# Gated linear attention with decays as per-token factors, grown block by block, two chunks per step

## The chip, the cores and the metric

The kernel runs on one core of a Trainium2 chip. The metric is the device time of one execution in microseconds (us), taken as the median of several timed runs. The core's engines are TensorE (PE in the rows; PEld is its loading of weights), VectorE (DVE), ScalarE (ACT), Pool (POOL) and SyncE (SP), which here only issues transfers. Each engine works through its own queue in order.

## The reference

One layer over 256 context tokens and 1024 latent tokens, width 1024. After a modulated norm one projection of 3616 columns feeds two groups of four heads: gated linear attention (GLA) in both directions, and differential attention. Their outputs are normed by head, gated, and projected back. The change is in GLA alone. In one direction, with queries q, keys k (64 features a head), values v (128), and log decays g, the reference computes over a chunk, starting from a state s:

```python
z_f = lr_f @ w_alpha[0] + b_alpha[0]
g_f = log_sigmoid(z_f) / 16.0                    # per token, head and feature; g_b the same for backward
b = cumsum(g, axis=1)
o_inter = einsum('bchk,bhkv->bchv', q * exp(b), s)
decay = where(causal, exp(minimum(b[:, :, None] - b[:, None, :], 0.0)), 0.0)
att = einsum('bthk,btshk,bshk->bhts', q, decay, k)
o_intra = einsum('bhts,bshv->bthv', att, v)
s_new = exp(b_last)[..., None] * s + einsum('bshk,bshv->bhkv', k * exp(b_last - b), v)
```

The output is `o_inter + o_intra`; the backward direction is the same over the flipped sequence, and the two are added. The decay differs by feature, so `att` isn't one product: between tokens t and s each feature has a factor of its own.

## The kernel before

The work is laid out with features (or tokens) on the 128 partitions, float32 throughout; projections are made as three products of rounded parts (hi x hi, hi x lo, lo x hi). Ten chunks of 128 tokens, 0 and 1 the context's, 2 to 9 the latents'.

The program has these stages. `START` is a hand-written list: modulation, norm of the input, first projections. Three `mix` calls follow, each with a pattern of letters from `MIX`: a letter m is a step of a projection (some 6 products of 512 columns or 12 of 256), a and b a step of what goes beside it. Mix 0 has q and gv projections, beside them `decays` (from the low-rank projection to summed log decays, kept in DRAM as `z_d`) and `modgate`. Mix 1 has four gate units, beside them `pass_a` (the forward state of each chunk, to `sf_d`) and loads of cached keys and values. Mix 2 has dv, dk and dq projections and four gate units, beside them `pass_b` (both directions' outputs, from the last chunk to the first), then the context's differential attention (`prompt`) and the first scores. Then a pipeline written out by hand (`ORDER`) does the differential attention of the latents, with the output projection at its end. The order of work in the mixes follows the patterns, with small shifts by the scheduler that places the instructions.

`pass_b` treats a chunk by levels, `LEVELS` = 64, 32, ..., 1: at level B, pairs of tokens that lie in one block of 2B but in different halves of it. For each level `decay` subtracts the summed log decay at the block's middle (line 825) and takes exponentials (lines 830, 831), which are at most 1 on either side; `weight` multiplies them into keys and queries (line 846); `product` gives 4 heads' 128 x 128 products from 64 features each (line 864, two levels to one PSUM tile `lv`, of which there is one); `select` copies the first into `att` and then, by a mask, each level's own places (line 873). The diagonal is an eighth level, by a sum over features (line 859). `ends` makes the decays towards the chunk's ends, with queries and decays loaded a second time with halves of the partitions exchanged, so that one tile holds both directions' states and 128 rows contract both at once. `output` (line 908) adds state and `att` products in one PSUM tile; squares, their mean (lines 925, 926), scaling (930), gate (933), parts (937, 938) and the store follow. A step of `pass_b` is two levels of one chunk: four steps a chunk. Decays are issued three steps ahead of their product and weights two. `ENG` says which of these operations go to Pool.

```python
for i, (c, lp_) in enumerate(steps):
    x = chunk(c)
    x.product(lp_)
    x.select(lp_)
    ...
    if last is not None:
        finish(last, lp_, x)
    stage("weight", i + 2)
    stage("decay", i + 3)
```

Of the kernel before, what the change touches and what calls it, by code (L numbers as in the profile page):

```python
# [12 lines left out]
F32 = mybir.dt.float32  # L13
# [3 lines left out]
ALU = mybir.AluOpType  # L17
# [16 lines left out]
LEVELS = [64, 32, 16, 8, 4, 2, 1]  # L34

# columns of the table of per-feature vectors
# [9 lines left out]
class Ctx:  # L46
    pass

# [15 lines left out]
def stagger(gens, lag):  # L64
    """each generator starts lag steps after the one before it"""
# [70 lines left out]
# the steps up to the first units' end, see Start; XV, XL, WE: what the vector engine (or for weights' rounding,  # L136
# the scalar engine) takes of a step
# [34 lines left out]
def body(tc, nc, I, O, ctx):  # L172
# [27 lines left out]
    # DRAM scratch  # L200
    kq_d = dram.tile([NCH, P, 4, P], F32, name="kq_d")
    z_d = dram.tile([NCH, P, 4, P], F32, name="z_d")
# [26 lines left out]
    with psum:  # L229
# [11 lines left out]
        def load_unit(u):  # L241
            """hi and lo parts of a unit"""
# [23 lines left out]
            # the condition, in two parts, and beside zeros  # L266
# [7 lines left out]
            # lambda of the differential heads, on every partition  # L274
# [13 lines left out]
        class Start:  # L288
            """the steps of the modulation and of the first units; START lists them in their order"""
# [5 lines left out]
            # scale (part 0) and shift (part 1) of half of the features: i = half, part, pair of k tiles  # L295
# [45 lines left out]
            # token tile t of the input: loaded, normalised  # L341
# [1237 lines left out]
```

## Time and profile before

| what | value |
|---|---|
| timed runs | 998.23 us median (997.64, 998.23, 1001.78) |
| span of the profiled execution, first to last instruction | 994.7 us |
| median of the runs above that span | 3.5 us |
| TensorE, VectorE, ScalarE, Pool busy | 905.1, 705.4, 508.5, 457.0 us |
| mean granted clock of TensorE | 0.983 of full |

The profiled execution has no time of its own beside its span; 3.5 us is what the median of the timed runs lies above it. Busy time is the union of an engine's instructions. Overlapping products count once, and a matmul's printed duration is its passage through the array, so the distance between starts is what one costs. The granted clock is the share of full speed (2.4 GHz) that TensorE was given; its other level is 1.2 GHz.

### The profile page before, as it was taken

The numbers are of one execution on the slowest core, as the hardware profiler recorded it, in microseconds if no ns is written. First come the engines' busy times: TensorE is split into PE (matmuls) and PEld (weight loads), VectorE is DVE, ScalarE is ACT, GpSimd is POOL, SyncE is SP. The second block draws the span as 40 slices with busy tenths as digits, with TensorE's granted clock in tenths as the row PEclk, the third lists the DMA queues.
The fourth block names the chain that finished last, engine by engine and source line by source line (L and its number), as shares of the span: only waits on it lengthen the run. The fifth ranks groups of instructions, "written<-read, shape, count | busy, mean of one in ns | idle before, by whom it ended". The sixth has DMA issues, their size and how long they took to land. (4 is left out here: it accounts for less than half of the span.)

```text
span 994.7 us, 16162 instructions
## 1 busy us (share of the span) xinstructions
PE 905.1 (91%) x5780; PEld 765.4 (77%) x5780; DVE 705.4 (71%) x995; ACT 508.5 (51%) x1066; POOL 457.0 (46%) x378
## 2 busy tenths in 40 slices
PE   6889999999997898788799999799988889999997
PEld 1489888977887797676688888688777767888886
DVE  3788954235889979999976746899888889822223
ACT  2454354356734445444432556687767777832121
POOL 0354223224415345454433100188899999752221
PEclk9989999999999999989999999999999999999999
DMA  8842744588644535343355654263445325237751
GB/s 281 325 149 65 241 146 128 178 287 294 219 134 134 178 120 156 123 159 123 134 161 178 194 171 133 69 178 124 143 159 143 97 80 177 67 112 217 239 169 63
DMA packets 143361, 160.30 MB, mean 161 GB/s; under 512 B 11049, under 2 KB 107945, under 8 KB 143281
## 3 DMA queue, kind: packets, MB, share of 16 engines
q1 hardware_dynamic: 143280, 159.28, 50.2%
q8 instruction: 45, 0.74, 0.3%
q14 instruction: 36, 0.29, 0.1%
HBM read 107.97 MB, written 51.26 MB: 160 GB/s over the span
## 5 line engine op out<-in xcount | busy, mean ns | idle before, releaser
L446 PE MATMUL acc<-hhi,w_hi 128*128 128x512 f32 (+1 forms) x440 | 160.0, 364 | 0.0
L448 PE MATMUL acc<-hhi,w_lo 128*128 128x512 f32 (+1 forms) x440 | 156.7, 356 | 0.0
L447 PE MATMUL acc<-hlo,w_hi 128*128 128x512 f32 (+1 forms) x440 | 156.7, 356 | 0.0
L1179 DVE TENSOR_REDUCE sm<-sc 128x1 f32<-128x1536 f32 x60 | 105.0, 1751 | 11.4 <-PE sc L1172 11.3
L1172 PE MATMUL sc<-ks,q 128*128 128x512 f32 x360 | 96.7, 404 | 3.0 <-ACT p L1184 3.0
L1184 ACT ACTIVATE p<-sc,sm 128x1536 f32<-128x1536 f32 x60 | 92.4, 1539 | 10.3 <-DVE sm L1179 7.1
L521 PE MATMUL acc<-w_hi,hhi 128*128 128x256 f32 x320 | 93.9, 293 | 3.4 <-DVE gt L650 1.7
L1223 POOL TENSOR_TENSOR aTl<-aT,aTh 128x512 fp32r<-128x512 f32 x64 | 91.7, 1433 | 4.9
L446 PEld LDWEIGHTS acc<-hhi,w_hi 128*128 128x128 f32 x440 | 84.5, 192 | 12.3 <-issue 1.4
L448 PEld LDWEIGHTS acc<-hhi,w_lo 128*128 128x128 f32 x440 | 84.2, 191 | 12.1
L447 PEld LDWEIGHTS acc<-hlo,w_hi 128*128 128x128 f32 x440 | 84.4, 192 | 10.7 <-issue 0.2
L522 PE MATMUL acc<-w_lo,hhi 128*128 128x256 f32 x320 | 91.9, 287 | 0.0
L523 PE MATMUL acc<-w_hi,hlo 128*128 128x256 f32 x320 | 91.8, 287 | 0.0
L1220 POOL TENSOR_SCALAR aTh<-aT 128x512 fp32r<-128x512 f32 x59 | 61.2, 1038 | 42.2 <-ACT aT L1209 39.9
L1172 PEld LDWEIGHTS sc<-ks,q 128*128 128x128 f32 x360 | 63.4, 189 | 13.9 <-ACT p L1184 3.3
L521 PEld LDWEIGHTS acc<-w_hi,hhi 128*128 128x128 f32 x320 | 62.5, 195 | 9.0 <-issue 3.3
L864 PE MATMUL lv<-w 64*128 64x128 f32 x560 | 43.0, 290 | 27.9 <-DVE att L873 27.8
L1209 ACT ACTIVATE aT<-tp 128x512 f32<-128x512 f32 x80 | 47.8, 598 | 39.1 <-PE tp L1203 18.2
L830 ACT ACTIVATE e<-d 128x256 f32<-128x256 f32 x70 | 29.6, 422 | 70.8 <-DVE d L825 57.0
L1203 PE MATMUL tp<-ident,p 128*128 128x128 f32 x360 | 54.7, 274 | 11.8 <-ACT aT L1209 11.8
L864 PEld LDWEIGHTS lv<-w 64*128 64x128 f32 x560 | 35.6, 191 | 38.2 <-issue 23.0
L1389 PE MATMUL sc<-woh,oh 128*128 128x512 f32 (+1 forms) x168 | 65.0, 387 | 0.0
(363 smaller groups left out, 2434.0 us busy)
## 6 DMA issues: line engine op xcount, KB each, us to landing
w_raw<-w_u SPq DMA_DIRECT2D x29, 512.0 KB, 4.1
oh<-oh_d SPq DMA_DIRECT2D x20, 512.0 KB, 6.0
wm<-w_mod SPq DMA_DIRECT2D x16, 512.0 KB, 5.0
q<-qs_d SPq DMA_DIRECT2D x64, 128.0 KB, 2.9
ks<-ks_d SPq DMA_DIRECT2D x4, 1536.0 KB
vs<-vs_d SPq DMA_DIRECT2D x8, 768.0 KB, 7.8
xt<-x_all SPq DMA_DIRECT2D x10, 512.0 KB, 8.2
x<-x_all SPq DMA_DIRECT2D x10, 512.0 KB, 3.7
```

Source lines behind the costliest of these rows:

```text
L446: T.matmul(ps, w_h, hhi[bi][:, kt, ts], start=kt == 0, stop=False)
L447: T.matmul(ps, w_h, hlo[bi][:, kt, ts], start=False, stop=False)
L448: T.matmul(ps, w_l, hhi[bi][:, kt, ts], start=False, stop=kt == KT - 1)
L521: T.matmul(ps, h_h, w_h, start=kt == 0, stop=False)
L522: T.matmul(ps, h_h, w_l, start=False, stop=False)
L523: T.matmul(ps, h_l, w_h, start=False, stop=kt == KT - 1)
L864: T.matmul(self.lv[:, h % 2, i, h // 2], kk[r:r + 64, h // 2], qq[r:r + 64, h // 2], start=True, stop=True)
L1172: T.matmul(sc[:, k0:k0 + w], self.q[:, a, sub, qt * P:(qt + 1) * P], self.ks[:, sub, k0:k0 + w], start=a == 0, stop=a == 1)
L1179: V.tensor_reduce(out=self.sm[qt][:, sub:sub + 1], in_=self.sc[qt, sub], op=ALU.max, axis=AX.X, negate=True)
L1184: A.activation(p_, self.sc.pop((qt, sub)), AF.Exp, bias=sm[:, sub:sub + 1], accum_out=self.s0[:, qt:qt + 1] if sub == 0 else sm[:, 2:3])
L1223: eng.tensor_tensor(out=lo, in0=full, in1=hi.bitcast(F32), op=ALU.subtract)
L1389: T.matmul(ps, oh[:, 0, m], woh[m][:, cs], start=m == 0, stop=False)
```

## The change

Factors instead of summed logs: `decay` now takes the exponential of each token's log decay and keeps it in `e_d` (both directions), with a scan from the right (forward only) for the products to the chunk's end that `pass_a` needs, so that `pass_a` has no exponentials left.

`pass_b` is rewritten around a `Pair` of chunks, 2p and 2p+1, and the levels go up: `LEVELS` = 1, 2, ..., 64. `first` multiplies the queries by each token's own factor. `tree` forms the products of factors over blocks of 2, 4, ..., 128 tokens. Keys and queries of both directions lie in one tile `w`; between level B and 2B, `grow(B)` multiplies, in place, the half of the tokens that gets farther from the block's end by the product of the neighbour block: one operation for the keys of both directions, one for the queries. For levels up to 64 the two directions' grown halves of the keys are copied into one contiguous tile `kk`. `product(s)` has 8 products (4 heads, 2 chunks) per step, with the queries read as alternating runs of B from the two directions; step 0 is the diagonal, an ordinary product scaled by 2. After the last level `w` holds what the states and the output need, so `ends`, the swapped loads and the diagonal's parts are gone. Forward and backward states are products of 64 rows each. The tile `lv` is now double, and the output's PSUM tile `op` is one of the two; the PSUM pool `psX` has one buffer (`XB` = 1) instead of two. Most SBUF tiles of the linear attention have one buffer; squares and parts share the tags `sq`, `hi` and `lo`. A pair takes eight steps, its end is done in the next pair's steps. `MIX`, `ORDER`, `START` and everything else stay. Lines that only lose a comment are left out here, and so is the reassignment of buffers in `modgate` and `prompt`.

```diff
-LEVELS = [64, 32, 16, 8, 4, 2, 1]
+LEVELS = [1, 2, 4, 8, 16, 32, 64]
-XB = 2
+XB = 1
...
+def view(t, r0, rn, off, dims):
+    row = t.ap[0][0]
+    return bass.AP(t.tensor, t.offset + r0 * row + off, [(row, rn), *dims])
...
-        psL = psG.enter_context(tc.tile_pool(name="psL", bufs=1, space=PSUM, reuse_waits="tile"))
-        psO = psG.enter_context(tc.tile_pool(name="psO", bufs=1, space=PSUM, reuse_waits="tile"))
+        psL = psG.enter_context(tc.tile_pool(name="psL", bufs=2, space=PSUM, reuse_waits="tile"))
...
-        gp = gla.enter_context(tc.tile_pool(name="gp", bufs=2, reuse_waits="tile"))
+        gp = gla.enter_context(tc.tile_pool(name="gp", bufs=1, reuse_waits="tile"))
...
         def decay(bi, c0, n):
...
+                    G.tensor_tensor(out=mn, in0=mn, in1=la, op=ALU.subtract)
+                    ex = gp.tile([P, 4, 129], F32, name="ex", tag="ET"[pr])[:, :nch]
+                    G.memset(ex[:, :, P:P + 1], 0.0)
+                    A.activation(ex[:, :, 0:P], mn.rearrange("p (c t) -> p c t", t=P), AF.Exp, scale=1.0 / 16)
+                    S.dma_start(e_d[ch0:ch0 + nch, :, dp, :].rearrange("c p t -> p c t"), ex[:, :, 0:P])
+                    if dr == 0:
+                        to = gp.tile([P, 4, 129], F32, name="to", tag="vq"[pr])
...
+                        V.tensor_tensor_scan(out=t1[:, n1 - 1::-1], data0=e1[:, n1:0:-1], data1=m1[:, n1 - 1::-1],
+                                             initial=0.0, op0=ALU.mult, op1=ALU.add)
...
+                        S.dma_start(e_d[ch0:ch0 + nch, :, 4 + pr, :].rearrange("c p t -> p c t"), to)
...
+        TOFF = {B: 1024 - 2048 // B for B in (2, 4, 8, 16, 32, 64, 128)}
+        class Pair:
+            GS, AS, CS = 1024, 512, 256
+            def __init__(self, p):
+                self.p = p
+                cs = slice(2 * p, 2 * p + 2)
+                self.w = gp.tile([P, 2, 2, 2, 2 * P], F32, name="w", tag="W", bufs=2)
+                self.q = gp.tile([P, 2, 2 * P], F32, name="q")
+                self.e = gp.tile([P, 2, 2, 2 * P], F32, name="e", tag="E")
...
+            def first(self):
+                out = view(self.w, 0, P, self.AS, [(self.GS - self.AS, 2), (1, 512)])
+                V.tensor_tensor(out=out, in0=self.q.rearrange("p c t -> p (c t)").unsqueeze(1).broadcast_to([P, 2, 512]),
+                                in1=view(self.e, 0, P, 512, [(-512, 2), (1, 512)]), op=ALU.mult)
+            def tree(self):
+                self.t = gp.tile([P, 1024], F32, name="t", tag="T")
+                old, n = self.e.rearrange("p a c t -> p (a c t)"), 1024
+                for B in (2, 4, 8, 16, 32, 64, 128):
+                    o2, n = old.rearrange("p (m two) -> p m two", two=2), n // 2
+                    new = self.t[:, TOFF[B]:TOFF[B] + n]
+                    V.tensor_tensor(out=new, in0=o2[:, :, 0], in1=o2[:, :, 1], op=ALU.mult)
+                    old = new
...
+            def grow(self, B):
+                t, o, n = (self.e, 0, 512) if B == 1 else (self.t, TOFF[B], 512 // B)
+                run = [(2 * B, n // 2), (1, B)]
+                tot = lambda off, step: view(t, 0, P, o + off, [(step, 2), (2, n // 2), (0, B)])
+                k = view(self.w, 0, P, 0, [(self.GS + self.AS + B, 2), *run])
+                V.tensor_tensor(out=k, in0=k, in1=tot(1, n - 1), op=ALU.mult)
+                if B < 64:
+                    self.kk = gp.tile([P, 512], F32, name="kk", bufs=2)
+                    A.activation(self.kk.rearrange("p (m two j) -> p m two j", two=2, j=2 * B),
+                                 view(self.w, 0, P, 0, [(4 * B, n // 4), (self.GS + self.AS + 2 * B, 2), (1, 2 * B)]), AF.Copy)
+                q = view(self.w, 0, P, self.AS, [(self.GS - self.AS + B, 2), *run])
+                V.tensor_tensor(out=q, in0=q, in1=tot(n + 1, -(n + 1)), op=ALU.mult)
+            def product(self, s):
+                self.lv = psL.tile([P, 2, 512], F32, name="lv", tag="lv")
+                B = 2 ** (s - 1) if s else 0
+                for i in range(2):
+                    for pr in range(2):
+                        for par in range(2):
+                            r, o = par * 64, i * self.CS + pr * P
+                            k = view(self.w if s < 2 else self.kk, r, 64, o, [(1, P)])
+                            if s == 0:
+                                q = view(self.q, r, 64, o, [(1, P)])
+                            else:
+                                q = view(self.w, r, 64, o + self.AS, [(2 * B, 64 // B), (self.GS - self.AS + B, 2), (1, B)])
+                            T.matmul(self.lv[:, par, i * 256 + pr * P:i * 256 + (pr + 1) * P], k, q, start=True, stop=True)
+            def select(self, s):
+                if s == 0:
+                    self.att = gp.tile([P, 2, 2, 2, P], F32, name="att", bufs=2)
+                    A.activation(self.att.rearrange("p a c r t -> p a (c r t)"), self.lv, AF.Copy, scale=2.0)
+                else:
+                    V.copy_predicated(out=self.att.rearrange("p a c r t -> p (a c r) t"),
+                                      data=self.lv.rearrange("p a (x t) -> p (a x) t", t=P),
+                                      mask=masks[:, s - 1].unsqueeze(1).broadcast_to([P, 8, P]))
...
+            def output(self):
+                self.op = psL.tile([P, 2, 512], F32, name="op", tag="lv")
...
+            def square(self, i):
+                op = self.op[:, :, i * 256:(i + 1) * 256]
+                self.sq = gp.tile([P, 512], F32, name="sq")
+                A.activation(self.sq.rearrange("p (a b) -> p a b", a=2), op, AF.Square)
+                self.sqh = gp.tile([P, 512], F32R, name="sqh", tag="hi")
+                G.tensor_scalar(out=self.sqh, in0=self.sq, scalar1=1.0, scalar2=0.0, op0=ALU.mult, op1=ALU.add)
+                self.sql = gp.tile([P, 512], F32R, name="sql", tag="lo")
+                G.tensor_tensor(out=self.sql, in0=self.sq, in1=self.sqh.bitcast(F32), op=ALU.subtract)
...
         def pass_b():
+            x, last = Pair(NCH // 2 - 1), None
+            x.first()
+            yield
+            finish = (lambda y: y.turn(), lambda y: y.states(), lambda y: y.output(), lambda y: y.square(1),
+                      lambda y: y.norm(1), lambda y: y.square(0), lambda y: y.norm(0), lambda y: None)
+            while x is not None:
+                nxt = None
+                for s in range(8):
+                    x.product(s)
+                    if s == 0:
+                        x.tree()
+                    else:
+                        x.grow(2 ** (s - 1))
+                    x.select(s)
+                    if last is not None:
+                        finish[s](last)
+                    if s == 3:
+                        x.bring()
+                        if x.p:
+                            nxt = Pair(x.p - 1)
+                    if s == 6 and nxt is not None:
+                        nxt.first()
+                    yield
+                last, x = x, nxt
+            for s in range(7):
+                finish[s](last)
+                if s % 2:
+                    yield
```

## Rows read from the trace of the kernel before

**Rows 1.** Busy time by stretch: bounds, length, engines, granted clock, DMA share, GB/s

```profile
core 0: us, PE busy (x) PEld busy (x) DVE busy (x) ACT busy (x) POOL busy (x), PEclk, DMA share, GB/s
259.00:526.00 267.00, 231.80 (x1784) 200.58 (x1784) 242.68 (x361) 122.01 (x291) 113.52 (x82) 0.96 0.47 149
529.00:599.00 70.00, 69.75 (x403) 61.00 (x402) 39.42 (x69) 35.17 (x87) 9.20 (x6) 1.00 0.57 180
100.00:200.00 100.00, 98.36 (x686) 88.66 (x684) 52.59 (x75) 39.67 (x80) 29.91 (x31) 1.00 0.56 175
200.00:257.00 57.00, 55.79 (x324) 45.01 (x323) 31.29 (x58) 36.88 (x88) 23.02 (x20) 1.00 0.85 280
```

**Rows 2.** TensorE's longest waits, 255 to 530 us: total, times, longest

```profile
PE lv L864 <- DVE att L873: 27.8, 18, 3.3
```

**Rows 3.** TensorE in order of time, 304 to 311.7 us: start, length, instruction

```profile
304.19 1.16 PE L864 MATMUL lv<-w 64*128 64x128 f32 x16
305.29 0.49 PE L908 MATMUL op<-qq,Sfb 128*128 128x128 f32 x2
...
306.95 0.39 PE L908 MATMUL op<-att,vc 128*128 128x128 f32 x2
310.35 1.16 PE L864 MATMUL lv<-w 64*128 64x128 f32 x16 [3.01 <-DVE att L873]
```

**Rows 4.** VectorE by line, 259 to 526 us: busy, mean ns, idle before

```profile
L846 DVE TENSOR_TENSOR w<-e,kq 128x512 f32<-128x512 f32 x55 | 52.0, 953 | 1.4 <-ACT e L831 1.2
L873 DVE COPY_PREDICATED att<-masks,lv 128x512 f32<-128x512 int32 x70 | 51.1, 730 | 6.0 <-ACT att L871 2.9 <-PE lv L864 1.6 <-PE lv L859 1.3
L825 DVE TENSOR_TENSOR d<-zc 128x512 f32<-128x512 f32 x46 | 40.3, 879 | 1.3 <-ACT e L831 1.1
L884 DVE TENSOR_TENSOR qq<-e,kq 64x256 f32<-64x256 f32 x20 | 12.3, 614 | 0.3
L894 DVE TENSOR_TENSOR qq<-qb,qs 64x256 f32<-64x256 f32 x18 | 12.2, 679 | 0.8 <-PE op L908 0.6
L933 DVE TENSOR_TENSOR og<-og,gtc 128x512 f32<-128x512 f32 x9 | 11.4, 1271 | 0.0
L762 DVE SCALAR_TENSOR_TENSOR Sfb<-Sfb,et,u 64x128 f32<-64x128 f32 x28 | 8.9, 344 | 0.5
...
L930 DVE TENSOR_TENSOR og<-op,sq 128x512 f32<-128x512 f32 x9 | 6.2, 683 | 1.1 <-ACT sq L928 1.1
```

**Rows 5.** Single lines over the whole span: duration in ns, min/median/max

```profile
L846 DVE TENSOR_TENSOR w<-e,kq x60: 665/684/2848, 249.2 to 501.1; 128x512 f32<-128x512 f32 x60
L873 DVE COPY_PREDICATED att<-masks,lv x70: 703/731/759, 266.1 to 515.7; 128x512 f32<-128x512 int32 x70
L886 DVE TENSOR_TENSOR ks<-e,kq x10: 411/426/2491, 268.8 to 505.5; 128x256 f32<-128x256 f32 x10
L253 DVE TENSOR_TENSOR w_lo<-w_raw,w_hi x13: 1201/1218/2290, 102.2 to 581.9; 128x1024 fp32r<-128x1024 f32 x13
```

**Rows 6.** Pool by line, 259 to 526 us

```profile
L825 POOL TENSOR_TENSOR d<-zc 128x512 f32<-128x512 f32 x18 | 23.3, 1303 | 69.4 <-ACT e L831 53.9 <-DVE og L930 12.0 <-issue 3.5
...
L846 POOL TENSOR_TENSOR w<-e,kq 128x512 f32<-128x512 f32 x10 | 16.0, 1604 | 7.5 <-ACT vhi L579 5.6 <-issue 1.5
L919 POOL TENSOR_TENSOR sql<-sq,sqh 128x512 fp32r<-128x512 f32 x10 | 15.4, 1536 | 1.7 <-DMA oh_d<-olo 0.8 <-DMA pq<-qs_d 0.5
L938 POOL TENSOR_TENSOR olo<-og,ohi 128x512 fp32r<-128x512 f32 x9 | 13.3, 1474 | 19.3 <-ACT ohi L937 19.3
```

**Rows 7.** ScalarE: one line by duration as in rows 5, then lines 259 to 526 us

```profile
L830 ACT ACTIVATE e<-d x70: 398/418/453, 247.5 to 500.1; 128x256 f32<-128x256 f32 x70
...
L927 ACT ACTIVATE sq<-ms,cst 128x512 f32<-128x512 f32 x9 | 6.1, 681 | 4.8 <-PE ms L926 4.7
...
L937 ACT ACTIVATE ohi<-og 128x512 fp32r<-128x512 f32 x9 | 5.7, 632 | 6.8 <-DVE og L933 5.2 <-DMA pvs<-vs_d 1.6
L928 ACT ACTIVATE sq<-sq 128x512 f32<-128x512 f32 x9 | 5.7, 630 | 0.3
```

**Rows 8.** Transfers by line: count, KB each, us from issue to landing

```profile
oh_d<-olo SPq DMA_DIRECT2D x10, 256.0 KB, 4.1
```

More of the change, by code (lines that the diff above doesn't have):

```diff
@@ L739, in state_f, with rows @@
[L739 to L763 removed]
+        def rows(par):
+            return slice(par * 64, par * 64 + 64)
@@ L767, in pass_a @@
             for c in range(NCH - 1):
-                kq, z, v = load_chunk(c, 0)
-                tt = gp.tile([P, 2], F32, name="tt")
-                V.tensor_scalar(out=tt, in0=z[:, 0:2, P - 1], scalar1=1.0 / 16, scalar2=None, op0=ALU.mult)
-                ks = gp.tile([P, 2, P], F32, name="ks")
-                for pr in range(2):
-                    A.activation(ks[:, pr], z[:, pr], AF.Exp, scale=-1.0 / 16, bias=tt[:, pr:pr + 1])
-                G.tensor_tensor(out=ks, in0=ks, in1=kq[:, 0:2], op=ALU.mult)
@@ L782, in pass_a @@
                 yield
-                yield from state_f(ks, v, cur, et, new)
+                tp = psX.tile([P, 512], F32, name="ktp", tag="aux")[:, :256]
+                for pr in range(2):
+                    T.transpose(tp[:, pr * P:(pr + 1) * P], ks[:, pr * P:(pr + 1) * P], ident)
+                A.activation(kt_, tp, AF.Copy)
+                yield
+                u = psX.tile([P, 512], F32, name="u", tag="aux")[:, :256].rearrange("p (a b) -> p a b", a=2)
+                for h in range(4):
+                    T.matmul(u[rows(h % 2), h // 2], kt_[:, h * 64:(h + 1) * 64], v[:, h * P:(h + 1) * P], start=True, stop=True)
@@ L784, in pass_a @@
+                if cur is None:
+                    V.tensor_copy(new, u)
+                else:
+                    for pr in range(2):
+                        V.scalar_tensor_tensor(out=new[:, pr], in0=cur[:, pr], scalar=totf[:, c, pr:pr + 1], in1=u[:, pr],
+                                               op0=ALU.mult, op1=ALU.add)
                 cur = new
@@ L942, in pass_b @@
         def pass_b():
-            order = list(range(NCH - 1, 1, -1)) + [1, 0]
-            chunks = {}
-            steps = [(c, lp_) for c in order for lp_ in range(4)]
-            def chunk(c):
-                if c not in chunks:
-                    chunks[c] = Chunk(c)
-                return chunks[c]
-            def stage(f, i):
-                if i < len(steps):
-                    c, lp_ = steps[i]
-                    for li in (lp_ * 2, lp_ * 2 + 1):
-                        getattr(chunk(c), f)(li)
@@ L959, in finish @@
-            def finish(x, lp_, now=None):
-                if lp_ == 0:
-                    x.output()
-                elif lp_ == 1:
-                    if x.c != 2:
-                        new = now.st if x.c else gp.tile([P, 2, 2, P], F32, name="Sfb", tag="Sf")
-                        x.add = state_b(x.kb, x.v, None if x.c == 1 else x.st, x.et, new)
-                        advance(x.add, 1)
-                        if x.c == 0:
-                            x.new = new
-                elif lp_ == 2:
-                    if x.c != 2:
-                        advance(x.add)
-                        if x.c == 0:
-                            for par in range(2):
-                                S.dma_start(O["nsb"][fwd(par)].rearrange("p (a b) -> p a b", a=2), x.new[bwd(par), par])
-                else:
-                    x.norm()
@@ L978, in pass_b @@
-            for i in range(3):
-                stage("decay", i)
-                if i < 2:
-                    stage("weight", i)
-            yield
-            last = None
-            for i, (c, lp_) in enumerate(steps):
-                x = chunk(c)
-                x.product(lp_)
-                x.select(lp_)
-                if lp_ == 1:
-                    x.states()
-                if last is not None:
-                    finish(last, lp_, x)
-                stage("weight", i + 2)
-                stage("decay", i + 3)
-                if lp_ == 0:
-                    x.bring()
-                if lp_ == 1:
-                    x.ends()
-                if lp_ == 3:
-                    last = x
-                yield
@@ L1007, in decays @@
                 yield from decay(bi, c0, n)
-            swapped(btsw, btot)
         prompt_o, gated = [], set()
```

346 lines of the change are left out of this document (121 added, 225 removed).

## Prediction

> **What bounds the kernel now.** I first looked at busy time by stretch. From 100 to 257 us, while the first projections, the decay factors and the forward states are made, TensorE is busy for all but 2.9 of 157 us; from 529 to 599 us, after the linear attention, for all but 0.25 of 70 [rows 1]. The stretch from 259 to 526 us, in which `pass_b` runs beside projections, is different: TensorE 231.8 of 267 us, VectorE 242.7 (91%), and the granted clock 0.96 [rows 1]. So TensorE idles for 35.2 us there, and a mean clock of 0.96 takes another 0.04 x 267 = 10.7 us. Next, the waits say for whom: 27.8 us in 18 waits of the level products (line 864) for the masked copy on VectorE (line 873) that frees their PSUM tile [rows 2]. In order of time one of these is seen whole: 16 products in 1.16 us, the output's products, then 3.01 us of nothing until the copy is done [rows 3]. The copy is late because its queue is full. So this stretch is bound by VectorE and the rest around it by TensorE; a change to the linear attention is worth at most what TensorE loses here, 35.2 + 10.7 = 46 us, and perhaps 1 to 2 us of the 2.9.
>
> **What VectorE does there.** The rows of the linear attention in this stretch are led by the multiplication of exponentials into keys and queries (52.0), the masked copy (51.1) and the subtraction of block middles (40.3) [rows 4]; with the smaller rows they make 216 us, and 26.5 us of the 242.7 are projections' evacuations. A part is waiting inside the instructions: a multiplication of 512 columns has a median of 684 ns and a mean of 953 in the stretch [rows 4, 5], while the masked copy, which reads PSUM, stays within 703 to 759. Pool is at work for 113.5 of the 267 us [rows 1], and I read the excess as VectorE waiting beside it. Over the 148 two-input operations of lines 846, 825, 884, 894 and 933 the mean over the median of their size makes some 37 us, 0.25 us each [rows 4, 5].
>
> **The change, part by part.** Two chunks now make one pair, so five pairs take the place of ten chunks, and a level's operation covers 1024 columns of both chunks where one of a chunk covered 512. Prices come from the medians: 422 to 426 ns at 256 columns, 684 at 512, 1218 at 1024, thus about 0.16 us and 1.03 ns a column [rows 5].
>
> Removed on VectorE, for two chunks: 14 masked copies of 512, ten or so subtractions, 12 multiplications, the diagonal's product and its two parts, end decays, swapped queries; 216 / 5 = 43 us for each two chunks. Added for a pair: `first`, one multiplication of 1024 columns, 1.2 us; `tree`, seven halving multiplications from 512 to 8 columns and a small copy, 2.3 us; `grow`, two multiplications of 512 columns at each of seven levels, 14 x 0.684 = 9.6 us; seven masked copies of 1024 columns, at 0.731 + 0.53 = 1.26, 8.8 us; four state updates at 0.344, 1.4 us; two times scaling and gating at 0.683 + 0.684, 2.7 us. That is 26 us a pair, 130 in all. The waiting beside Pool stays for 24 two-input operations a pair; Pool loses its subtractions and multiplication (23.3 + 16.0) and so falls from 113.5 to some 74 us, and 0.25 us shrinks in that proportion (74 of some 240 against 113.5 of 267) to 0.18: 120 x 0.18 = 22 us [rows 6]. VectorE's new work in the stretch is 130 + 22 + 26.5 = 178 us against 242.7.
>
> The uncertain price is `grow`. It reads and writes in place with steps of two blocks, and no VectorE row of before shows a strided output of this size. Below, it costs what a contiguous one does, 0.684; above, I take twice that, 1.37, which adds 48 us. The nearest row is ScalarE's exponential of half blocks, whose input and output are strided from runs of 64 down to single elements: 398 to 453 ns over all levels [rows 7]. Length of run makes no difference there, so I take 0.684 and keep 1.37 for the range.
>
> ScalarE loses the exponentials of the levels (140 of about 0.42 us, 59 us) and gains six copies of 512 columns at 0.63 and one evacuation of 1024 a pair, some 25 us; at 122 of 267 busy it sets no end. In the first stretch it gains twelve exponentials of at most 512 columns, 7.6 us, VectorE loses six scans, and SyncE's queue gets six stores more; TensorE at 98.4 of 100 us covers this, and uncovered it would cost the 7.6 us. The forward pass loses its exponentials and half of its loads; TensorE there has 1.2 us to gain [rows 1], I count nothing.
>
> TensorE: 128 half-height level products a pair at 1.16 / 16 us each against 112 and eight of the diagonal, +0.3 us. The output's state term becomes 32 half-height products, and 16 full-height ones stay: 2 x 1.16 + 2.05 = 4.4 us against 2 x 2.05 = 4.1 [rows 3]. If the half-height ones don't overlap they cost 2.05 for 16: +2 us. Between +3 and +12 us in all, I take 3, since they alternate halves and banks as the level products do. So TensorE's work at full clock is 231.8 - 10.7 + 3 = 224 us.
>
> **What is late next.** Once VectorE needs 178 us, TensorE sets the pace, but not alone. Before, the levels were independent and their weights were made two steps ahead; now a level's queries are multiplied in place, after the products that read them and before the next level's: 1.16 + 0.68 us from products to products at the least, and 178 / 40 = 4.5 us of VectorE in a mean step. The pattern that interleaves the work is the old one: of its first 44 linear-attention steps 7 have no projection step behind them and 11 have one, so TensorE's step is then some 2 or 3 us and it waits. To price this I use the two kinds of stretch: at a VectorE share of 0.56 TensorE loses 0.25 of 70 us, at 0.91 it loses 46 of 267 [rows 1]. At 178 / 241 = 0.74 a straight line gives 23 us. Waiting usually grows faster near the full share, which says less; the closed chain says more. I take 17 us, ends 1 and 23.
>
> **The sum.** 224 + 17 = 241 us where 267 were: 26 us less. The work behind, TensorE-bound, starts that much earlier. The profiled span of 994.7 becomes 968.7; the median of the runs, 998.2, lies 3.5 us above the span, so 972.
>
> **A rule that speaks against it.** The level products now take their queries as alternating runs of one block from two places, single elements at the first level; every moving operand of before is contiguous, so no row shows what this costs. The Trainium skill, "SBUF — State Buffer", section Specifications (TRN2), says that a read wants at least two hits in a 16-byte line for full bandwidth and pays for each move to a new line; by it the first level's products would be slowed, and no run here shows it yet.
>
> **The rivals.** (a) *The new waits take most of it back.* The norms of a pair's two chunks come two steps apart and share single buffers. From the end of the first one's mean product to the second's: 0.68 + 0.63 (exponentials), 0.68 + 1.27 (scaling, gating), 0.63 + 1.47 (parts), then the store of the low part lands 4.1 us later, and the second's low square takes 1.54 [rows 4, 6, 7, 8]: 11.0 us, against two steps of 6 us. It just fits; 3 us late in each pair, and in the tail where no projection step stands between, adds some 20 us: 985 to 997. For it: the single buffers; against: such waits cost TensorE nothing before. (b) *Broken runs slow TensorE.* At half pace in the first level it is 5 x 1.16 = 6 us; at a quarter there and half in the second, 5 x (3.5 + 1.2) = 23 us: 978 to 995. For it: each element then lies away from the one before; against: nothing in the profile. The rule of the Trainium skill cited above ("SBUF — State Buffer", Specifications (TRN2)) would act through this rival. (c) *Slower.* If the in-place strided multiplications are dear, VectorE stays the bound. Without `grow` it needs 178 - 48 = 130 us; it passes 242.7 when one of the 70 costs 1.6 us, 2.3 times its price; at 2 us it needs 270, and at today's share of 0.91 the stretch takes 297: 1028. For it: no row; against: ScalarE's strided row. (d) *Nothing changes*, because another engine or the queue of loads holds the stretch: ScalarE and Pool are at 46% and 43%, transfers at 0.47 [rows 1], so little speaks for it.
>
> **How the numbers follow.** Less than 0.5% (5 us) can't be told from no change. My forecast with its own range, 956 (nothing lost but 1 us, plus the 2.9 before) to 988 (23 us of waits and 12 of products), 62%; (a) 16%, of which 6 within 0.5%; (b) 6%; (c) 11%; (d) 5%. Faster 0.62 + 0.10 + 0.06 = 0.78, same 0.11, slower 0.11. The range runs from 952, TensorE nearly unbroken, to 997, which takes in (a), (b) and leaves (c) out.
>
> **What would show it.** In the profile of the changed kernel: VectorE near 180 us between the first level product and the last norm, that stretch near 240 us, clock 0.98 or above, the wait of level products for the masked copy gone or under 5 us. `grow`'s multiplications at a median of 0.68 to 0.70, masked copies at 1.26, 16 level products in 1.1 to 1.2 us at every level. If TensorE waits instead for the parts of the square or for `grow`, (a) is right; if first-level products take 2 us, (b); if `grow` takes over 1.4 us, (c). I am wrong if VectorE falls as said and the span doesn't.

## The result, and the profile after

The median of four runs is 984.67 us (980.46 to 987.1), beside 999.6 us for the kernel before on the same chip: a ratio of 0.985 with a 95% interval of 0.9813 to 0.9886. The change gains some 15 us; 26 were forecast, a time of 972. The profiled execution, the fastest of the four, took 980.46 us; its span is 978.4, 16.3 us less than before; the forecast span was 968.7. So 9.7 us of the miss of 12.7 lie in the span; the rest is that the median lies 6.3 us above the profiled span, where I had put 3.5.

Where did the 16.3 us come from? The projections' products are the same in both kernels and come in the same order, so one of them can be found in both traces, and the stretches between four such products hold the same work. Busy time by stretch, bounded by these products, first of before and then of after (columns as in [rows 1]):

```profile
core 0: us, PE busy (x) PEld busy (x) DVE busy (x) ACT busy (x) POOL busy (x), PEclk, DMA share, GB/s
0.00:118.70 118.70, 101.25 (x591) 74.82 (x592) 88.61 (x158) 48.96 (x111) 39.04 (x36) 0.96 0.63 216
118.70:203.99 85.29, 83.65 (x606) 75.42 (x604) 35.23 (x52) 34.74 (x72) 27.26 (x28) 1.00 0.51 156
203.99:260.15 56.16, 54.95 (x325) 44.45 (x323) 33.35 (x56) 36.63 (x88) 25.44 (x20) 1.00 0.84 280
260.15:600.14 339.99, 304.54 (x2203) 264.66 (x2202) 284.65 (x435) 159.63 (x384) 123.17 (x88) 0.97 0.49 154
600.14:994.70 394.56, 360.75 (x2063) 306.07 (x2061) 263.52 (x297) 228.52 (x415) 242.11 (x208) 1.00 0.44 135
```

```profile
0.00:116.98 116.98, 101.15 (x591) 75.00 (x592) 85.82 (x156) 48.13 (x111) 39.10 (x35) 0.96 0.65 218
116.98:205.19 88.21, 85.11 (x604) 76.59 (x602) 33.90 (x51) 37.85 (x74) 25.16 (x26) 0.98 0.53 159
205.19:265.95 60.76, 56.06 (x327) 44.29 (x325) 19.55 (x38) 30.13 (x55) 23.10 (x19) 1.00 0.78 259
265.95:584.59 318.64, 303.07 (x2317) 263.41 (x2315) 206.24 (x314) 116.79 (x230) 79.05 (x56) 0.99 0.50 156
584.59:978.40 393.81, 362.16 (x2063) 307.08 (x2061) 262.32 (x297) 228.23 (x415) 244.21 (x208) 0.99 0.44 135
```

Read the lengths against each other: -1.7, +2.9, +4.6, -21.4, -0.8. The stretch of the changed loop gave 21.4 us, close to the 26 of the forecast, and the two stretches in front of it, in which the decays and the forward pass are made, took 7.5 of them back. (The first 117 us hold little that was changed, two of the twelve steps of the decays, from 104 us on; in the kernels below their length varies from 117.0 to 119.9 us, so 1.7 us there say little.)

In the long stretch TensorE idled for 339.99 - 304.54 = 35.5 us before and for 15.6 after, while VectorE's work fell from 284.7 to 206.2. In the bounds of [rows 1], from the first level product to the last norm's product, the stretch is 257 us where 241 were forecast; but it ends further along the projections' products than it did, so the comparison above is the fairer one:

```profile
264.00:521.00 257.00, 241.45 (x1965) 209.21 (x1964) 172.31 (x255) 82.22 (x149) 70.31 (x50) 0.99 0.49 153
```

TensorE's waits from 100 to 540 us (total, times, longest) answer to [rows 2]; the wait for the masked copy, 27.8 us before, is now 0.7:

```profile
PE lv L831 <- DVE w L816: 6.6, 7, 2.9
PE ms L918 <- POOL sqh L910: 4.5, 4, 1.6
PE ktp L732 <- POOL fa L723: 4.5, 4, 1.5
PE acc L528 <- ACT kqst L477: 2.4, 1, 2.4
PE ms L919 <- POOL sql L912: 2.2, 4, 1.2
PE u L857 <- ACT kt L850: 1.5, 1, 1.5
PE lv L831 <- DVE att L838: 0.7, 2, 0.3
```

The prices, as in [rows 5]: the strided multiplications of the keys (line 810) and queries (816), and the masked copy of both chunks (838):

```profile
L810 DVE TENSOR_TENSOR w<-w,t x30: 669/692/1301, 280.9 to 494.0; 128x512 f32<-128x512 f32 x30
L816 DVE TENSOR_TENSOR w<-w,t x30: 665/692/1029, 282.7 to 495.2; 128x512 f32<-128x512 f32 x30
L838 DVE COPY_PREDICATED att<-masks,lv x35: 1286/1325/1354, 277.3 to 495.8; 128x1024 f32<-128x1024 int32 x35
```

And TensorE in order of time, the products of the diagonal and of blocks of 1, 2 and 4 tokens, 16 each:

```profile
264.86 1.16 PE L831 MATMUL lv<-q,w 64*128 64x128 f32 x16
275.05 1.59 PE L831 MATMUL lv<-w 64*128 64x128 f32 x16
279.63 1.23 PE L831 MATMUL lv<-w,kk 64*128 64x128 f32 x16
283.85 1.16 PE L831 MATMUL lv<-w,kk 64*128 64x128 f32 x16
```

At single elements the 16 take 0.43 us longer, at runs of two 0.07, at runs of four nothing.

**The clock.** A single drop in the trace of after lasts some 3.4 us at half of full speed, the lower of its two levels (1.2 of 2.4 GHz), which takes 1.7 us. One stands behind TensorE's waits for a second norm, between 333.9 and 336.7 us:

```profile
332.00:336.00 4.00, 2.17 (x24) 1.75 (x23) 3.31 (x6) 1.23 (x2) 2.08 (x3) 1.00 0.83 250
336.00:340.00 4.00, 3.72 (x18) 3.42 (x18) 2.17 (x4) 1.70 (x3) 0.69 (x1) 0.60 0.00 0
340.00:344.00 4.00, 4.00 (x35) 4.00 (x34) 1.11 (x3) 1.01 (x2) 1.29 (x1) 0.97 0.71 212
```

TensorE was busy for 2.17 of 4 us, and in the next stretch the granted clock is 0.60. Added up over stretches of 4 us (length times what the granted clock lacks of 1), the clock took 10.3 us of the long stretch before (as much as six such drops) and 3.4 after (two). This counts TensorE's idle time too; over its busy time alone it is 9.4 and 3.0.

### The profile page after: what moved, and what is told of

It is laid out like the page before. It is cut to its first block, busy times and chain, and to the rows that moved or that the text cites. A ratio compares the mean times of both kernels' runs of the same rounds, so it can differ in the third digit from the quotient of the medians.

```text
span 978.4 us, 15886 instructions
## 1 busy us (share of the span) xinstructions
PE 907.6 (93%) x5894; PEld 766.4 (78%) x5894; DVE 607.8 (62%) x853; ACT 461.1 (47%) x882; POOL 410.6 (42%) x344
## 4 chain that ended last, share of the span: by engine, by line
PE 51%; POOL 13%; DVE 11%; issue 10%; ACT 7%; DMA 6%; SPq 1%; POOLq 0%; ACTq 0%; DVEq 0%
PE acc L452 4%; PE acc L453 4%; PE acc L454 4%; PE sc L1347 4%; PE sc L1348 4%; PE sc L1349 4%; PE acc L528 3%; PE acc L530 3%; PE acc L529 3%; POOL aTh L1178 3%; PE lv L831 3%; ACT p L1142 3%; PE mp L324 3%; POOL wol L1311 2%; POOL woh L1310 2%
## 5 line engine op out<-in xcount | busy, mean ns | idle before, releaser
L1181 POOL TENSOR_TENSOR aTl<-aT,aTh 128x512 fp32r<-128x512 f32 x64 | 93.7, 1464 | 4.9
L1347 PE MATMUL sc<-woh,oh 128*128 128x512 f32 (+1 forms) x168 | 65.0, 387 | 0.0
L1349 PE MATMUL sc<-woh,oh 128*128 128x512 f32 (+1 forms) x168 | 64.6, 384 | 0.0
L1348 PE MATMUL sc<-wol,oh 128*128 128x512 f32 (+1 forms) x168 | 64.6, 384 | 0.0
L1192 PE MATMUL ov<-aTl,vs 128*128 128x256 f32 x192 | 56.3, 293 | 8.3 <-POOL aTl L1181 7.7
```

The source lines that it names most:

```text
L1347: T.matmul(ps, oh[:, 0, m], woh[m][:, cs], start=m == 0, stop=False)
L1348: T.matmul(ps, oh[:, 0, m], wol[m][:, cs], start=False, stop=False)
L1349: T.matmul(ps, oh[:, 1, m], woh[m][:, cs], start=False, stop=m == 7)
```

## The experiments

In the table the stretches are those between the same products: the decays' (88.21 us after), the forward pass's (60.76), the long one (318.64); then what the clock took of the long one, and what is left without it. "Ratio" is against the kernel before as timed beside that kernel on the same chip; since the chips differ, ratios compare better than medians. The columns from the span on are from one profiled execution each; the forward stretches of e4 and e5 hold a drop of the clock too.

| kernel | median us, ratio (95%) | span | decays | forward | long | clock | long less clock |
|---|---|---|---|---|---|---|---|
| before | 999.6 | 994.7 | 85.29 | 56.16 | 339.99 | 10.3 | 329.7 |
| after | 984.67, 0.985 (0.981 to 0.989) | 978.4 | 88.21 | 60.76 | 318.64 | 3.4 | 315.2 |
| e1 multiplication on VectorE | 980.93, 0.985 (0.980 to 0.990) | 976.7 | 87.63 | 58.42 | 320.14 | 5.2 | 315.0 |
| e2 contiguous query | 981.22, 0.984 (0.980 to 0.989) | 975.5 | 87.97 | 60.16 | 315.64 | 3.4 | 312.2 |
| e3 square's own buffers | 988.47, 0.990 (0.986 to 0.993) | 987.5 | 87.93 | 61.32 | 326.05 | 10.3 | 315.8 |
| e4 split keys and queries | 979.62, 0.982 (0.977 to 0.988) | 982.1 | 88.70 | 62.71 | 317.97 | 5.2 | 312.8 |
| e5 norm two steps | 986.27, 0.987 (0.983 to 0.992) | 986.7 | 88.76 | 63.70 | 322.23 | 6.8 | 315.4 |
| e6 one ahead | 984.77, 0.987 (0.983 to 0.991) | 980.9 | 88.80 | 59.42 | 320.34 | 5.1 | 315.2 |
| e7 dose, after | 993.65, 0.998 (0.994 to 1.001) | 986.4 | 88.57 | 59.85 | 326.31 | 6.8 | 319.5 |
| e8 dose, before | 1032.89, 1.035 (1.030 to 1.040) | 1030.0 | 85.26 | 54.86 | 375.65 | 29.0 | 346.6 |
| e9 second norm later | 981.51, 0.983 (0.980 to 0.987) | 983.6 | 88.67 | 60.02 | 321.40 | 6.8 | 314.6 |
| e10 four buffers | 975.12, 0.977 (0.974 to 0.980) | 970.7 | 89.52 | 56.33 | 313.55 | 1.7 | 311.8 |
| e11 e9 and e10 | 975.96, 0.977 (0.974 to 0.981) | 974.4 | 88.39 | 55.09 | 316.89 | 5.2 | 311.7 |
| e12 e10, decay on VectorE | 972.28, 0.973 (0.970 to 0.976) | 971.1 | 86.06 | 55.06 | 317.49 | 5.2 | 312.3 |

**Does VectorE set the pace? (e7, e8)** The same dose of VectorE work in both kernels:

```diff
                     V.copy_predicated(out=self.att..., data=self.lv..., mask=...)
+                    for par in range(2):          # before: once, on its 512 columns
+                        a = self.att[:, par].rearrange("p c r t -> p (c r t)")
+                        V.tensor_tensor(out=a, in0=a, in1=a, op=ALU.max)
```

> The changed kernel, with two more VectorE operations of 512 columns (each the maximum of the weights with themselves) behind every masked copy: 70 in all, some 0.68 us each, 48 us more in a stretch in which VectorE has 172 of 257 us busy. If VectorE no longer sets the pace there: the time grows by 4 to 20 us. If it still does (its share is low only because it waits in turn with TensorE): by 35 us or more.

> The kernel before, with one more VectorE operation of 512 columns behind every masked copy: 70 in all, some 0.68 us each, 48 us more in a stretch in which VectorE has 243 of 267 us busy, the same dose as in the changed kernel. If VectorE set the pace there, as the prediction took it: the time grows by 35 to 60 us. If the pace was set by TensorE and by the way from product to masked copy, and VectorE had room: by under 20 us.

The long stretch of each, after with the dose and then before with it:

```profile
266.11:592.42 326.31, 307.71 (x2316) 265.85 (x2315) 255.09 (x384) 117.10 (x230) 84.03 (x56) 0.98 0.49 152
```

```profile
259.99:635.64 375.65, 321.61 (x2203) 277.55 (x2201) 330.24 (x506) 160.58 (x384) 124.83 (x89) 0.92 0.45 141
```

In the changed kernel 48.9 us more of VectorE work made the stretch 7.7 us longer; in the kernel before 45.6 us more made it 35.7 longer. Part of both is the clock's, which fell more often: 18.7 of the 35.7 us and 3.4 of the 7.7, so without it the dose cost 16.9 us before and 4.3 after. Not all of a dose shows even before, so VectorE wasn't the only limit there; it was the main one, and now is hardly one. Both expectations of the first theory held, that of e8 at its lower edge (35.8 us where 35 to 60 were expected).

**The loss in front of the loop (e1, e6, e10).** TensorE's transposes in the forward pass wait 4.5 us for GpSimd's multiplication of a chunk's keys by its decays. Is GpSimd late, or the load?

```diff
-                G.tensor_tensor(out=ks, in0=k, in1=to, op=ALU.mult)
+                V.tensor_tensor(out=ks, in0=k, in1=to, op=ALU.mult)
```

> The forward pass's multiplication of k by the decays to the chunk's end is on VectorE instead of GpSimd, and nothing else is changed. If it is GpSimd's turn that the transposes wait for (4.5 us in 4 waits in the profile after): the four waits shrink to under 1 us together, the first level product starts 3.5 to 4.5 us before its 264.9 us, and the time is 980 to 982 us. If it is the load of k and of the decays that is late and GpSimd only passes the wait on: the waits stay at 3.5 us or more, now put down to VectorE or a DMA, and the time stays within 1 us of 984.7.

The waits shrank to 2.5 us (1.8 and 0.7), not under 1, and the stretch by 2.3 us: neither of the two theories as it was put. A shorter operation (0.43 us for 0.73) on another queue is worth about half; the other half is in front of it. The trace of after shows the chain for one chunk, SyncE's two loads and GpSimd's multiplication behind them:

```profile
206.06 0.37 SPq L720 DMA_DIRECT2D fa<-kq_d  x1
206.47 0.45 SPq L721 DMA_DIRECT2D fa<-e_d  x1
210.02 0.73 POOL L723 TENSOR_TENSOR fa<-fa 128x256 f32<-128x256 f32 x1 [0.57 <-DMA fa<-e_d]
```

It is 3.5 us from the second load's issue to its use, and the loads can start only when one of two buffers is free. Before, there were two buffers as well, but keys, decays, product and values were tiles of their own, and the keys' buffer was free again with the multiplication; in the changed kernel one tile `fa` holds them all and is free only after the state's product. In the traces the next load follows either at once, the first two rows from before, the others from after:

```profile
201.25 0.73 POOL L774 TENSOR_TENSOR ks<-ks,kq 128x256 f32<-128x256 f32 x1 [1.28 <-ACT ks L773]
202.01 0.32 SPq L711 DMA_DIRECT2D kq<-kq_d  x1
```

```profile
211.47 0.66 PE L737 MATMUL u<-fa 128*64 128x128 f32 x8
212.17 0.32 SPq L720 DMA_DIRECT2D fa<-kq_d  x1
```

So the decays' load, the later of the two that the exponential or the multiplication needs, came 5.0 to 7.6 us ahead of the multiplication before (five chunks from 201 us on) and 2.4 to 5.8 us after. e6 issues load and multiplication a step earlier on the same two buffers; e10 does so with four, made by halving the tiles (keys, decays, product and turned keys in one half, the values in a buffer that is idle then), with the keys and queries of a pair in two tiles as in e4.

```diff
             for c in range(NCH - 1):
...
                 yield
+                if c + 1 < NCH - 1:
+                    bring(c + 1)                  # the loads and the multiplication of the next chunk
                 tp = psX.tile(...)
```

> The forward pass loads and multiplies a chunk one step earlier, ahead of the state product of the chunk before it, still on GpSimd; nothing is left out. If the change's loss before the first level product is the late start of that multiplication: the transposes' waits (4.5 us in 4) fall under 1 us and the first level product starts 3 to 4.5 us before 264.9 us. If GpSimd is late because of its other work (the weights' halves), an earlier place in its queue pushes that instead: the start moves by less than 1.5 us and waits for GpSimd appear at the projections.

> The forward pass has four buffers for keys and decays instead of two (the halves of the tiles of e4, with its split keys and queries) and loads one chunk ahead. If the loss ahead of the first level product comes from the chain from a buffer that comes free through a load (3.2 us) and the multiplication: the transposes' waits (4.5 us in 4) fall under 1 us and the first level product starts 3 to 4.5 us before 264.9 us. If it is GpSimd's own lateness: the waits stay above 3 us, as with one chunk ahead on two buffers (3.7).

With two buffers the wait stayed at 3.7 us. With four it is gone from e10's waits (100 to 540 us), and the stretch of the forward pass is 56.33 us, the 56.16 of before:

```profile
PE lv L842 <- DVE att L849: 4.3, 5, 2.3
PE ms L929 <- POOL sqh L921: 4.0, 4, 1.3
PE acc L528 <- ACT kqst L477: 3.9, 1, 3.9
PE u L868 <- ACT kt L861: 1.9, 1, 1.9
PE ms L930 <- POOL sql L923: 1.5, 4, 0.5
```

So the loss of 4.6 us was the chain from a freed buffer through a load to the multiplication, not GpSimd's lateness alone. That it began with laying the tiles together follows from the traces above; two buffers of separate tiles in the changed kernel were not tried. e10 is also the first version whose interval (0.974 to 0.980) lies below the changed kernel's.

**The decays (e12).** The trace of after, 129 to 135 us: ScalarE's new exponential waits for GpSimd's subtraction, which waits for VectorE, and a weight's rounding and the copy that TensorE needs stand behind it.

```profile
130.79 0.74 DVE L551 TENSOR_SCALAR mn<-z,vecs 128x512 f32<-128x512 f32 x1
131.68 1.29 POOL L552 TENSOR_TENSOR mn<-mn,la 128x512 f32<-128x512 f32 x1 [1.93 <-DVE mn L551]
133.00 0.63 ACT L556 ACTIVATE ex<-mn 128x512 f32<-128x512 f32 x1 [2.94 <-POOL mn L552]
133.53 1.04 ACT L256 ACTIVATE w_hi<-w_raw 128x1024 fp32r<-128x1024 f32 x1
134.48 0.57 ACT L477 ACTIVATE kqst<-acc 128x512 f32<-128x512 f32 x1
135.11 0.39 PE L528 MATMUL acc<-w_hi,hhi 128*128 128x256 f32 x1 [2.43 <-ACT kqst L477]
```

```diff
-                    G.tensor_tensor(out=mn, in0=mn, in1=la, op=ALU.subtract)
+                    V.tensor_tensor(out=mn, in0=mn, in1=la, op=ALU.subtract)
```

> The kernel with four buffers for the forward pass and keys and queries in two tiles, and in it the decays' subtraction on VectorE, right behind VectorE's own operation on the same tile, instead of GpSimd. If the changed kernel's loss at 118 to 140 us comes from the new exponential, which waits on ScalarE for GpSimd's subtraction (2.9 us at 133.0 us) with the projection's copy behind it: TensorE's wait for that copy (2.4 us in the changed kernel, 3.9 us in this one without the edit) falls under 2 us, the clock no longer drops behind it, and the time falls by 1.5 to 4 us against the kernel without the edit (975.1). If the copy is late for the weights' split or the store of its buffer: the wait stays above 2 us and the time within 1 us.

The wait fell from 3.9 to 1.9 us (e12's row below; e10's stands above), the clock no longer dropped behind it, and the stretch went from 89.52 to 86.06 us: 2.2 of these 3.5 us are TensorE's busy time, which is the clock, and 1.3 its idle time.

```profile
PE acc L528 <- ACT kqst L477: 1.9, 1, 1.9
```

The span hardly moved (970.7 to 971.1), since the clock fell twice more in the long stretch (5.2 us for 1.7), where nothing was edited. By the timed runs, 972.28 us, it is the fastest kernel here, though its interval overlaps e10's. Before, TensorE waited 1.58 us at this place too, for the same copy, so in the trace of after the change's own part is 0.85 us of wait and the 1.7 us drop behind it. The drop isn't tied to the wait, though: in e3 and e9 the same wait (2.4 and 2.7 us) had none behind it, and their stretch took 87.93 and 88.67 us all the same, with smaller waits beside it (1.4 and 1.8 us in all, 0.6 in after). How much of the 2.9 us the exponential's place in the queue costs is therefore shown only in part.

**Broken runs (e2).**

```diff
-  q = view(self.w, r, 64, o + self.AS, [(2 * B, 64 // B), (self.GS - self.AS + B, 2), (1, B)])
+  q = view(self.w, r, 64, o + self.AS, [(1, P)] if s == 1 else [(2 * B, 64 // B), ...])
```

> The second of a pair's eight products (blocks of one token) reads one half of its queries as one run of 128 instead of alternating between the two halves token by token; the scores of that level are then those of the other half for every second token. If the alternating reads make TensorE slow (16 products in 1.59 us in the profile after, 1.16 us at the others): these 16 fall to 1.1 to 1.2 us, and the five pairs give back 2.1 us, 982 to 983 us. If it is something else of that step (the weights read for the last time, the multiplication on VectorE that runs beside it): they stay above 1.5 us and the time stays within 0.5 us.

Its products of blocks of one token, in order of time:

```profile
274.75 1.16 PE L831 MATMUL lv<-w 64*128 64x128 f32 x16
```

1.16 us for 1.59, and the long stretch 3.0 us shorter at the same loss to the clock, 2.15 of them these products. The alternating reads are the cause.

**The norms (e3, e5, e9).** From the first norm's products to the second's it is 9.4 us in the first three pairs and 11.5 in the last, and in these four TensorE waits (in the fourth pair it is 15.5, without a wait). Three attempts: buffers of their own for the rounded square and its rest (`tag="kt"`, `tag="g"`); the squares earlier, two steps ahead of their norms; the second norm a step later.

```diff
-  finish = (turn, states, output, square(1), norm(1), square(0), norm(0), None)
+  finish = (turn, states, output + square(1), None, norm(1) + square(0), None, norm(0), None)   # e5
+  finish = (turn, states, output, square(1), norm(1), square(0), None, norm(0))                 # e9
```

> The rounded square and its rest get buffers of their own (those of the turned keys and of the gate), so that they no longer wait for the stores of the gated output. If the norms wait because of the shared buffers (6.7 us of TensorE before the norm's products, 4.5 and 2.2): these waits fall under 2.5 us and the time is 980 to 982 us. If they wait because one step lies between the square and the norm, whatever the buffers (ScalarE's square, then two GpSimd operations in a row): the waits stay above 5 us and the time stays within 1 us of 984.7.

> Each norm comes two steps after its square instead of one (the first square right behind the output, the first norm and the second square two steps later, the second norm in its old place); nothing is left out. If it is the one step between that makes TensorE wait for GpSimd's rounded squares (6.7 us in the profile after, and the clock fell behind two of these waits, 1.7 us each): these waits fall under 2.5 us, the drops of the clock at 336 and 436 us are gone, and the time is 974 to 978 us. If the waits only move to the level products, as the same engines are late for those: TensorE's idle time between 264 and 521 us stays above 13 us and the time within 2 us of 984.7.

> The second norm of a pair (its two products and all behind them) comes one step later, in the last step of the next pair instead of the last but one; its square stays where it is, and no buffer is added. If TensorE waits there for the chain that the single buffers make out of the two norms (9.4 us from the first norm's products at 326.0 us to the second's at 335.4): the wait for GpSimd's rounded squares falls from 6.7 us under 3, the drops of the clock behind two of these waits (336 and 436 us, 1.7 us each) are gone, and the time is 975 to 980 us. If the output's sums, held one step longer, only move the wait: the level products of the last step and of the next pair's first wait 4 us or more in all, and the time is within 2 us of 984.7 or above it.

None gained clear of the noise. In e3 the waits stayed (5.8 and 2.6 us): the distance fell to 8.0 us in the first pair but rose to 9.9 in the second, since the gate's load now had to wait for the buffer it gave away (VectorE waits 4.7 us for it), and the clock took as much as four more drops. In e5 they stayed at 4.5 and 1.9, with the same 9.3 to 9.4 us between in the first three pairs: the square is late because its buffer is held until the first norm's result is split. In the trace of after it starts at 332.60 us, right behind that split on GpSimd, and its rounding then waits for the store of the high part (GpSimd idle for 1.8 us until then). My theory of the one step fell. In e9 the order on TensorE moved in the first pair alone; there the wait vanished (the second norm 16.2 us behind the first), and in the next two it stayed 9.4 and 9.5 us behind. Without the clock its long stretch is 0.6 us shorter. Whether a second set of buffers for the whole norm would pay was not tried.

**Keys and queries in two tiles (e4).**

```diff
-  self.w = gp.tile([P, 2, 2, 2, 2 * P], F32, name="w", tag="W", bufs=2)
+  self.wk = gp.tile([P, 2, 2, 2 * P], F32, name="wk", tag="W", bufs=4)
+  self.wq = gp.tile([P, 2, 2, 2 * P], F32, name="wq", tag="W", bufs=4)
```

> Keys and queries of a pair lie in two tiles instead of one, so that the multiplication of the keys need not wait for the product before it, which reads only the queries; all else is the same (the pool's tiles are halved to make room). If TensorE's wait for the grown queries (6.6 us in 7) comes from the keys' multiplication standing ahead of them behind the product: VectorE's wait ahead of the keys' multiplication (17.4 us in 14) falls under 8 us, TensorE's 6.6 us fall under 2.5, and the time is 979 to 982 us. If VectorE is late for its own load (the masked copies of 1.29 us): both waits change by less than a third and the time stays within 1.5 us of 984.7.

VectorE's wait ahead of the keys' multiplication fell from 17.4 to 5.2 us and TensorE's wait for the grown queries went; but 4.5 us of waits for the masked copy took its place, and VectorE's wait ahead of the queries' multiplication, which still follows the product, rose from 5.8 to 14.4 us. Net of the clock the long stretch is 2.4 us shorter: the first theory's mechanism, at half its size.

**Both together (e11).**

> Both of the edits before it in one kernel: the second norm a step later, the forward pass on four buffers and a chunk ahead, keys and queries in two tiles. If both reasons hold, their gains add, since they lie in different stretches: 970 to 976 us and TensorE idle under 10 us between the first level product and the last norm. If waits are only passed on from place to place: not under 980 us.

It gave what e10 gives (975.96 us, 311.7 us net of the clock against 311.8), and TensorE idled for 11.5 us between the first level product and the last norm, not under 10: the later norm adds nothing.

## Why the prediction came out as it did

- *VectorE bounds the stretch, TensorE the rest*: right for the stretch, shown by e8 and e7, with part of e8's cost being the clock's.
- *VectorE's new work, 178 us*: 172.3 measured. The strided multiplication was forecast at 0.684 us and has a median of 0.692, the masked copy 1.26 and 1.325. The waiting that was read as beside GpSimd, put at 22 us, is smaller: the means of the two multiplications, 0.747 and 0.705, lie close to the median (0.908 and 0.898 at the first level). Nor is the near hit of the total what it seems. The 26.5 us put down for the projections took the linear attention's rows, summed, 216 us, from a busy time in which overlapping operations count once. Summed alike, VectorE's rows of before are 216 us of linear attention and 49 of projections. After they are 133 (forecast 130 + 22), 50, and 4 of the context's differential attention: 187 in sum, 172.3 busy. So the waiting was put too high and the projections too low, and luck let the two cancel. Rival (c) is out.
- *TensorE's idle time, 35.2 to 17*: 15.6 in the long stretch. What waits there is what I named: `grow` (6.6 us) and the norms (6.7). The size is partly luck: the straight line gave 23 us, and 17 was a choice below it that no row fixed.
- *The clock's 10.7 us*: forecast to come back whole; 6.9 of 10.3 did, since two drops remain, each behind TensorE's waits for a second norm. The forecast had no term for drops behind the new waits.
- *TensorE's work, +3 us*: busy time less the clock's loss goes from 304.5 - 10.3 = 294.3 to 303.1 - 3.4 = 299.7, +5.4. The first level's broken runs are 2.15 of this. That is rival (b) in kind, at 0.5 us a pair (0.43 and 0.07) instead of 1.16 to 4.7. The Trainium skill, "SBUF — State Buffer", section Specifications (TRN2), asks for two hits in a 16-byte line for full bandwidth and charges for each move to a new one. The traces agree in kind: single elements cost 37% more, runs of two 6%, runs of four (16 bytes) nothing.
- Together 19.9 + 6.9 - 5.4 = 21.4 us for the 25.9 of the sum: 4.5 of the span's miss of some 9.7 us lie in the loop.
- *Decays and forward pass "counted as nothing"*: **this is the step that failed.** The text said that TensorE, at 98.4 of 100 us busy, covers the new exponentials, and saw only a gain of 1.2 us to be had in the forward pass, counted as nothing. The two stretches lost 7.5 us, 2.9 and 4.6, the larger part of the miss. That the text named 7.6 us for exponentials that are not covered is a coincidence. A busy TensorE covers nothing when it is the one that waits: the exponential went into ScalarE's queue ahead of a copy that TensorE needs, and the forward pass's load and multiplication came onto its path, since the one tile is free later than the separate ones of before. Nor did its loads halve: three remain for each chunk, with two thirds of the bytes. I had costed these edits by what each engine does in all, not by what stands behind each in its queue, which the prediction did for the loop. e10 gives the forward pass's part back. e12 takes the decays' stretch to 86.06 us, 0.8 above before, mostly by drops of the clock that did not come; what of that is the queue's stays open.
- Rival (a), single buffers: the chain was forecast at 11.0 us and is 9.4; it costs 6.7 us of waits, with the two drops of the clock (3.4 us) behind them, not the 20 us that would have made it the outcome.

## What to carry to other kernels

When a change takes load off the engine that sets the pace, cost its smaller edits elsewhere by queue and buffer: what the new instruction waits for, what stands behind it that the pacing engine needs, and which instruction is the last to hold each buffer. Two buffers that are free late are fewer than two that are free early. Compare two traces between instructions that both have; the stretch that was changed, and the places where its gain is lost, then come out by subtraction. A dose of extra work on one engine, the same before and after, tells whether it sets the pace more surely than its busy share.

## What the runs showed of the hardware

How often the clock falls decides more than most of these edits. The clock's loss in the long stretch comes in multiples of 1.7 us: as much as one to six drops in the versions of the changed kernel, while the same stretch net of the clock lies at 314.6 to 315.8 us in six whose loops differ in the norms at most (after, e1, e3, e5, e6, e9), at 312.2 in e2 and at 311.7 to 312.8 in the four with split tiles. Drops came behind idle time of TensorE, as at 333.9 us, but not behind every long wait: the longest of after, 2.9 us at 471.6, had none. What decides it stays open.
